# A first pair of feed-forward chunks by plain block products, with the input's sums made beside it

## The chip, the cores and the metric

One core of one Trainium2 chip runs the whole model. The metric is device time in microseconds (us); lower is better. All numbers are of the kernel before the change until the prediction ends.

## What is computed

The input x has 512 tokens of width 1024. It goes through two blocks of a first kind (feed-forward, attention mixture with pooling, feed-forward) and one block of a second kind (a mixing stage, then feed-forward). There are so five feed-forward layers, and each does this, with a width of 2816 between:

```python
def rmsnorm(x, g):
    xf = x.astype(jnp.float32)
    y = xf * lax.rsqrt(jnp.mean(xf * xf, axis=-1, keepdims=True) + NORM_EPS)
    return (y * g.astype(jnp.float32)).astype(x.dtype)

def swiglu(h, w_gate, w_up, w_down):
    return (jax.nn.silu(h @ w_gate) * (h @ w_up)) @ w_down
```

All data are float32, and the result is added to x (times 0.5 in the first four layers).

## The kernel before

x lies transposed in SBUF as eight tiles `x[0]` to `x[7]` of 128 channels by 512 tokens. TensorE multiplies in a 32-bit format that rounds, so every operand is split into a rounded high part and a low part (`wh`, `wl` for weights, `yh`, `yl` for the input), and one product is three matmuls: high by high, high by low, low by high. The high part is made on ScalarE (line 360 for weights), the low part on VectorE (line 368 for weights). The row factor of the norm is not put into the input: the sum of squares `ss` is made on the side (line 476, on POOL and VectorE), turned into a factor per token (`row_factor`: eight small matmuls `tst`, line 495, and eleven tiny VectorE steps, lines 484 to 497), spread over the partitions (`spread`: transposes `tbc`, line 506, and a copy into `rbc`, line 513), and multiplied into the gate and up results (line 575).

**A pair of chunks.** The width 2816 is 22 chunks of 128, taken in 11 pairs. For one pair, the weights (gate and up, two chunks) and the input (two halves of the 1024 channels, `x[0..3]` and `x[4..7]`, and two halves of the 512 tokens) form a 2 by 2 block product. It is done with seven half-size products, not eight, after Strassen and Winograd (`PRODUCTS`: W11, S1, S2, W12, S3, S4, W22). Each product is 24 matmuls of 256 columns (`product`, lines 628 to 630). For this the weights are summed on VectorE in `source` (lines 326, 330, 337, 341), and the input in `prep_a` (a difference of token halves for chunks 0 to 3, line 432) and `prep_b` (three sums `r` per chunk, lines 443 to 445, their high and low parts `rh`, `rl`, lines 447 and 450, and the split of chunks 4 to 7, lines 449 and 451). The seven results are put together by ScalarE snapshots (line 557), a ScalarE copy (line 595) and three VectorE adds (lines 606, 608, 610). Then `finish` scales a chunk by the row factor, applies SiLU, multiplies gate by up and splits the result into `ah`, `al`.

**The order.** `ffn_plan` lists the work: four phases of pairs, (0, 1), (2, 3, 4), (5, 6, 7), (8, 9, 10); the down-projections (`D`, eight per phase, line 600 adds them into x) of one phase are spread over the products of the next. The first phase so has two pairs with nothing beside them. The loop in `ffn` does one item after the other; after each it evacuates the item before and prepares weights two items ahead (`highs`, `lows`, `SPLIT = 2`). The row factor's statistics are issued after the third item, its spread after the fourth. A scheduler orders the instructions of each engine when the kernel is built, with the written order as priority; on the chip every engine then runs its queue in order.

**Where the input is prepared.** For the first layer `prep_a` and `prep_b` run ahead of everything. For layers behind a mixing stage, `prep_a` runs with the last output projection (`second`), and `prep_b` when the layer's pool opens (`layers`). The third layer follows a feed-forward layer directly: there both run as each x tile is finished (`next_ffn`).

**Buffers and queues.** Weights come by DMA on SyncE's queue into tiles `wr`, `wq`, `wd` (three buffers each); `wh` and `wl` have three buffers each, weight sums `wt` two, snapshots three. A feed-forward product writes one of PSUM's banks of tags x0, x1, x2, two buffers each.

Of the kernel before, what the change touches and what calls it, by code (L numbers as in the profile page):

```python
# [100 lines left out]
BLOCKS = {"W11": ((0, 0),), "S1": ((1, 0), (1, 1)), "W12": ((0, 1),)}  # L101

PHASES = ((0, 1), (2, 3, 4), (5, 6, 7), (8, 9, 10))
D_ORDER = (0, 4, 1, 5, 2, 6, 3, 7)


def ffn_plan():

    for ph, pairs in enumerate(PHASES):
        todo = [(ph, p, n) for p in pairs for n in PRODUCTS]  # L110
        ds = [(ph - 1, d) for d in D_ORDER] if ph else []
        for i, t in enumerate(todo):
# [107 lines left out]
def tile_blocks(tc, A, out):  # L220
# [3 lines left out]
    with (  # L224
# [46 lines left out]
        def home(m):  # L271

            j, _ = owner[m]
            name = PLAN[j][0]
            if name == "u":
                return "wr"
            if name in ("D", "W12"):
                return "wd"
            return "wq" if homes_of[j] % 2 else "wr"

        homes_of, n = {}, 0
        for j, (name, _) in enumerate(PLAN):
            if name == "u":
                n = 0
            elif name == "W11":
                n += 1
            homes_of[j] = n - 1
# [25 lines left out]
        def source(j):  # L313

            name, ws = PLAN[j]
            m = first_load[j]
            if name in ("u", "D"):
                return raws[m], ws[0], [m]
# [33 lines left out]
        def high(j):  # L352

            if PLAN[j][0] not in ("u", "W11") and state["ffn"] is None:
                return False
            if not loads(j):
                return False
            src, n, free = source(j)
            h = wspl.tile([P, 1024], F32R, name="wh", tag="wh")
            ACT.activation(h[:, :n], src[:, :n], AF.Copy)  # L360
            made[j] = src, n, free, h
            return True
# [64 lines left out]

        def prep_a(c, g):

            t = small.tile([P, S], F32, name="sq", tag="sq", bufs=2)  # L430
            ACT.activation(t, x[c], AF.Copy, scale=gain(g, c))
            V.tensor_sub(t[:, HALF:], t[:, :HALF], t[:, HALF:])
            h, l = new_pair(c)
            ACT.activation(h, t, AF.Copy)
            V.tensor_sub(l, t, h.bitcast(F32))  # L435

        def prep_b(c, g):

            b = state["ffn"].tile([P, 4, HALF], F32, name="b4", tag="cc", bufs=2)
            r = state["ffn"].tile([P, 4, HALF], F32, name="r3", tag="cc", bufs=2)[:, :3]  # L440
            ACT.activation(b[:, 0:2], x[c + 4], AF.Copy, scale=gain(g, c + 4))
            ACT.activation(b[:, 2:4], x[c], AF.Copy, scale=gain(g, c))
            V.tensor_sub(r[:, 1], b[:, 1], b[:, 3])
            V.scalar_tensor_tensor(r[:, 0], r[:, 1], -1.0, b[:, 2], op0=ALU.mult, op1=ALU.subtract)
            V.scalar_tensor_tensor(r[:, 2], r[:, 0], -1.0, b[:, 0], op0=ALU.mult, op1=ALU.subtract)
            h, l = rest[c] = [state["ffn"].tile([P, 3, HALF], F32R, name=f"r{e}{c}", tag=f"r{e}{c}", bufs=1) for e in "hl"]
            ACT.activation(h, r, AF.Copy)  # L447
            yh, yl = new_pair(c + 4)
            ACT.activation(yh, b[:, 0:2], AF.Copy)
            V.tensor_sub(l, r, h.bitcast(F32))  # L450
            V.tensor_sub(yl, b[:, 0:2], yh.bitcast(F32))

# [87 lines left out]
        def operand(name, c):  # L540

            if name in ("W11", "S1"):
                t, j = pair[c], name == "S1"
            elif name in ("W12", "S4"):
                t, j = pair[c + 4], name == "S4"
            else:
                t, j = [p.rearrange("p a b -> p (a b)") for p in rest[c]], ("S2", "S3", "W22").index(name)
            return cut(t, slice(None), slice(j * HALF, (j + 1) * HALF))

        def ffn(coef, nxt):  # L550
            pool = state["ffn"]
# [15 lines left out]

            def finish(f):

                t = cc.pop(f)  # L570
                g, u, hl = t[:, :, 0], t[:, :, 1], []
                rb = got["rb"].rearrange("p (a b) -> p a b", a=2)

                def one():
                    V.tensor_tensor(t, t, rb.unsqueeze(2).to_broadcast([P, 2, 2, HALF]), op=ALU.mult)
                    ACT.activation(g, g, AF.Silu)
# [20 lines left out]
            def evac(t, o):  # L597
# [11 lines left out]
                elif n == "S4":  # L609
                    V.tensor_add(flat(chunk(2 * p), 1), o[n], snap["S2"])  # L610
                    finish(2 * p)
                elif n == "W22":
                    finish(2 * p + 1)

            def rest_of():
# [5 lines left out]
            def product(o, w, n, start):  # L621
                for j in range(2):
                    for c in range(4):
# [6 lines left out]
                        PE.matmul(oo, wl, xh, start=False, stop=c == 3, skip_group_check=True)  # L630

            before = None
            highs(state["next"] + 3)
            lows(state["next"] + 3)
            o = {}
            for i, t in enumerate(ffn_plan()):
                w = take()
                if len(t) == 2:
# [4 lines left out]
                    for k, f in enumerate(ks):  # L643
                        mm3(od, cut(w, slice(None), slice(k * P, (k + 1) * P)), a[f], k == 0, k == len(ks) - 1)
                    now = t, od
                else:
                    n = t[2]
# [16 lines left out]
                before = now  # L664
                if i == 2:
                    r = row_factor(sums["s"], D, "rf")
                if i == 3:
                    got["rb"] = spread(r)
            evac(*before)


# [134 lines left out]
        def mix(l, nxt):  # L806
            with tc.tile_pool(name="mix", bufs=2) as pool:
# [153 lines left out]
                def second(d, o):  # L961
                    first(d, o)
                    square_x(d)
                    if d < 4:
                        prep_a(d, nxt)

# [85 lines left out]
        def mix2(nxt):  # L1052
            with tc.tile_pool(name="mix2", bufs=2) as pool:
# [166 lines left out]
                with tc.tile_pool(name="at", bufs=2) as at:  # L1220
# [273 lines left out]
                    def second(d, o):  # L1494
# [4 lines left out]
                        if d < 4:  # L1499
                            prep_a(d, nxt)  # L1500

# [15 lines left out]
        def layers(g=None):  # L1517
            with tc.tile_pool(name="ffn", bufs=2) as pool:
                state["ffn"] = pool
                if g is not None:  # L1520
                    for c in range(4):
                        prep_b(c, g)
                yield
                state["ffn"] = None

        def next_ffn(g):
            def f(d):
                if d < 4:
# [22 lines left out]
        with layers():  # L1551
            for c in range(4):
                prep_a(c, G_FFN1)
                if c == 0:
                    ahead(1)
            ahead(2)
            for c in range(4):
                prep_b(c, G_FFN1)
# [3 lines left out]
            ffn(0.5, next_mix(G_MIX))  # L1562
        mix(0, G_FFN2)
        with layers(G_FFN2):
            ffn(0.5, next_ffn(G_FFN1 + 1))
            ffn(0.5, next_mix(G_MIX + 1))
        mix(1, G_FFN2 + 1)
        with layers(G_FFN2 + 1):
            ffn(0.5, next_mix(G_PROD))
        mix2(G_FFN3)  # L1570
        with layers(G_FFN3):
            ffn(1.0, square_d)
        rb = spread_out(row_factor(sums["s"], D, "rf"))
# [22 lines left out]
```

## Time and profile before

| what | us |
|---|---|
| median of three runs (2571.61 to 2573.69) | 2573.45 |
| the profiled execution | 2572.86 |
| its span, first to last instruction | 2571.1 |
| TensorE (PE) busy | 2475.6 |
| VectorE (DVE) busy | 2003.3 |
| ScalarE (ACT) busy | 1345.3 |
| GpSimd (POOL) busy | 343.9 |

Busy time is the union of the times of an engine's instructions. Matmuls overlap in TensorE's pipeline, so one matmul's duration says less than the distance between two starts. The granted clock is given as a share of 2.4 GHz: 0.50 is 1.2 GHz. A VectorE instruction of 512 columns takes about 0.7 us in the trace and the next one starts about 0.6 us after it began. In the trace's names `x<-yh,wh` is a feed-forward product from a split input chunk, `x<-rh,wh` one from a sum of the input, `dn` a down-projection, `mm` a product of a mixing stage.

### The profile page before, as it was taken

The numbers are of one execution on the slowest core, as the hardware profiler recorded it, in microseconds if no ns is written. First come the engines' busy times: TensorE is split into PE (matmuls) and PEld (weight loads), VectorE is DVE, ScalarE is ACT, GpSimd is POOL, SyncE is SP. The second block draws the span as 40 slices with busy tenths as digits, with TensorE's granted clock in tenths as the row PEclk, the third lists the DMA queues.
The fourth block names the chain that finished last, engine by engine and source line by source line (L and its number), as shares of the span: only waits on it lengthen the run. The fifth ranks groups of instructions, "written<-read, shape, count | busy, mean of one in ns | idle before, by whom it ended". The sixth has DMA issues, their size and how long they took to land.

```text
span 2571.1 us, 40560 instructions
## 1 busy us (share of the span) xinstructions
PE 2475.6 (96%) x16074; PEld 2248.3 (87%) x16074; DVE 2003.3 (78%) x2935; ACT 1345.3 (52%) x2120; POOL 343.9 (13%) x498
## 2 busy tenths in 40 slices
PE   6999999998999999999999998999999999799997
PEld 5999988887999989999988887999987887799996
DVE  8887764788887779877756789887768888888775
ACT  5444443676544456444444776444455775554442
POOL 1000014431000000000023531000013553000001
PEclk9999999998999999999999998999999999799999
DMA  4333232212333332333232112333233211333322
GB/s 146 114 102 103 72 100 90 58 34 86 99 103 105 105 108 82 103 109 105 77 91 79 42 50 96 114 101 103 73 109 99 88 34 42 99 107 103 97 70 76
DMA packets 73342, 229.78 MB, mean 89 GB/s; under 512 B 9536, under 2 KB 9920, under 8 KB 73152
## 3 DMA queue, kind: packets, MB, share of 16 engines
q1 hardware_dynamic: 73152, 227.19, 29.1%
q8 instruction: 126, 2.06, 0.3%
q14 instruction: 64, 0.52, 0.1%
HBM read 225.06 MB, written 2.10 MB: 88 GB/s over the span
## 4 chain that ended last, share of the span: by engine, by line
PE 84%; DVE 10%; ACT 3%; issue 2%; POOL 1%; DMA 0%; DVEq 0%; SPq 0%; ACTq 0%; POOLq 0%
PE x L629 14%; PE x L630 14%; PE x L628 14%; PE dn L404 8%; PE dn L405 7%; PE dn L406 7%; PE mm L404 4%; PE mm L405 4%; PE mm L406 4%; DVE wl L368 2%; PE ov L1015 2%; PE tp L997 2%; PE mm L754 1%; PE mm L755 1%; PE ov L1292 1%
## 5 line engine op out<-in xcount | busy, mean ns | idle before, releaser
L628 PE MATMUL x<-yh,wh 128*128 128x256 f32 x1760 | 507.1, 288 | 20.2 <-ACT wh L360 14.1
L629 PE MATMUL x<-yl,wh 128*128 128x256 f32 x1760 | 506.8, 288 | 13.6 <-DVE yl L435 7.9
L630 PE MATMUL x<-yh,wl 128*128 128x256 f32 x1760 | 505.7, 287 | 3.7 <-DVE wl L368 3.7
L360 ACT ACTIVATE wh<-wd 128x768 fp32r<-128x768 f32 (+2 forms) x270 | 242.8, 899 | 358.2 <-PE x L629 178.7
L628 PE MATMUL x<-rh,wh 128*128 128x256 f32 x1320 | 377.2, 286 | 14.8 <-ACT rh L447 10.0
L629 PE MATMUL x<-rl,wh 128*128 128x256 f32 x1320 | 376.9, 286 | 4.0 <-DVE rl L450 4.0
L630 PE MATMUL x<-rh,wl 128*128 128x256 f32 x1320 | 376.0, 285 | 0.8 <-DVE wl L368 0.8
L628 PEld LDWEIGHTS x<-yh,wh 128*128 128x128 f32 x1760 | 344.2, 196 | 25.8 <-ACT wh L360 14.8
L629 PEld LDWEIGHTS x<-yl,wh 128*128 128x128 f32 x1760 | 344.3, 196 | 19.9 <-DVE yl L435 9.7
L630 PEld LDWEIGHTS x<-yh,wl 128*128 128x128 f32 x1760 | 344.7, 196 | 4.9 <-DVE wl L368 4.9
L404 PE MATMUL dn<-ah,wh 128*128 128x512 f32 x880 | 343.9, 391 | 0.0
L405 PE MATMUL dn<-al,wh 128*128 128x512 f32 x880 | 343.8, 391 | 0.0
L406 PE MATMUL dn<-ah,wl 128*128 128x512 f32 x880 | 342.3, 389 | 0.0
L360 ACT ACTIVATE wh<-wr 128x1024 fp32r<-128x1024 f32 (+1 forms) x178 | 187.7, 1055 | 244.1 <-PE x L629 89.9
L476 POOL TENSOR_TENSOR ss<-ss,sq 128x512 f32<-128x512 f32 x48 | 70.1, 1460 | 1807.6 <-ACT sq L475 1794.6
L368 DVE TENSOR_TENSOR wl<-wd,wh 128x768 fp32r<-128x768 f32 (+2 forms) x270 | 276.4, 1024 | 42.8 <-ACT wh L360 40.2
L628 PEld LDWEIGHTS x<-rh,wh 128*128 128x128 f32 x1320 | 255.4, 193 | 19.6 <-ACT rh L447 12.1
L368 DVE TENSOR_TENSOR wl<-wr,wh 128x1024 fp32r<-128x1024 f32 (+1 forms) x166 | 207.8, 1254 | 73.7 <-ACT wh L360 72.9
L629 PEld LDWEIGHTS x<-rl,wh 128*128 128x128 f32 x1320 | 255.4, 193 | 7.4 <-DVE rl L450 5.7
L630 PEld LDWEIGHTS x<-rh,wl 128*128 128x128 f32 x1320 | 255.5, 194 | 1.0 <-DVE wl L368 1.0
L600 DVE SCALAR_TENSOR_TENSOR x<-dn,x 128x512 f32<-128x512 f32 x160 | 110.0, 688 | 115.3 <-PE dn L406 115.3
L406 PEld LDWEIGHTS dn<-ah,wl 128*128 128x128 f32 x880 | 165.2, 188 | 35.3
(334 smaller groups left out, 5221.3 us busy)
## 6 DMA issues: line engine op xcount, KB each, us to landing
wr<-in_w SPq DMA_DIRECT2D x175, 512.0 KB, 3.6
wd<-in_w SPq DMA_DIRECT2D x120, 384.0 KB, 3.1
wq<-in_w SPq DMA_DIRECT2D x78, 512.0 KB, 3.6
wd<-in_w SPq DMA_DIRECT2D x55, 512.0 KB, 3.6
wd<-in_w SPq DMA_DIRECT2D x40, 256.0 KB, 2.9
x<-in_xT SPq DMA_DIRECT2D x8, 256.0 KB, 5.9
out<-x SPq DMA_DIRECT2D x8, 256.0 KB, 2.0
bias<-in_consts SPq DMA_DIRECT2D x2, 448.0 KB, 4.0
```

The lines of the kernel that those rows point to most:

```text
L360: ACT.activation(h[:, :n], src[:, :n], AF.Copy)
L368: state["low"] = eng.tensor_sub(l[:, :n], src[:, :n], h[:, :n].bitcast(F32)).ins
L404: PE.matmul(o, w[0], xx[0], start=start, stop=False)
L405: PE.matmul(o, w[0], xx[1], start=False, stop=False)
L406: PE.matmul(o, w[1], xx[0], start=False, stop=stop)
L476: eng.tensor_add(sums["s"], sums["s"], sq)
L600: V.scalar_tensor_tensor(x[d], o, coef, x[d], op0=ALU.mult, op1=ALU.add)
L628: PE.matmul(oo, wh, xh, start=start and j == 0 and c == 0, stop=False, skip_group_check=True)
L629: PE.matmul(oo, wh, xl, start=False, stop=False, skip_group_check=True)
L630: PE.matmul(oo, wl, xh, start=False, stop=c == 3, skip_group_check=True)
L997: PE.transpose(o[:, i * P : (i + 1) * P], prob[h * TC + i][0][:, j * P : (j + 1) * P], ident)
L1015: PE.matmul(o, w, part, start=(j == 0 and n == 0), stop=(j == TC - 1 and n == 1))
```

## The change

The first pair of every layer (pair 0) is done by four plain block products, T11, T12, T21, T22, in place of the seven. Each takes one weight block as loaded, with no sums, and a whole split half of the input: 24 matmuls of 512 columns into two banks (gate and up). T11 and T12 add into the same two banks, which give the first chunk; T21 and T22 give the second. `finish` scales straight out of these banks. The input is now split whole for all eight chunks (`split`), and `sums_of` makes four sums per chunk, with their high and low parts; it is called in `ffn` after each of the first four items, or, for the layer behind a feed-forward layer, in `next_ffn`. The weights of T11, T12 and T21 may be prepared before the layer's pool is open. The row factor's statistics are issued after the first item and the spread after the second.

```diff
+PLAIN = ("T11", "T12", "T21", "T22")
+BLOCKS.update({f"T{i + 1}{j + 1}": ((i, j),) for i in range(2) for j in range(2)})
...
-        todo = [(ph, p, n) for p in pairs for n in PRODUCTS]
+        todo = [(ph, p, n) for p in pairs for n in (PRODUCTS if p else PLAIN)]
...
-            if name in ("u", "D"):
+            if name in ("u", "D") or name in PLAIN:
                 return raws[m], ws[0], [m]
...
-            if PLAN[j][0] not in ("u", "W11") and state["ffn"] is None:
+            if PLAN[j][0] not in ("u", *PLAIN[:3]) and state["ffn"] is None:
                 return False
...
-        def prep_a(c, g):
...
-        def prep_b(c, g):
...
+        def sums_of(c, g):
+
+            b1, b2 = (state["ffn"].tile([P, 2, HALF], F32, name="b", tag="snap", bufs=3) for _ in range(2))
+            r = state["ffn"].tile([P, 4, HALF], F32, name="r", tag="wt", bufs=2)
+            ACT.activation(b1, x[c], AF.Copy, scale=gain(g, c))
+            ACT.activation(b2, x[c + 4], AF.Copy, scale=gain(g, c + 4))
+            V.tensor_sub(r[:, 0], b1[:, 0], b1[:, 1])
+            V.tensor_sub(r[:, 2], b2[:, 1], b1[:, 1])
+            V.scalar_tensor_tensor(r[:, 1], b2[:, 1], -1.0, r[:, 0], op0=ALU.mult, op1=ALU.subtract)
+            V.scalar_tensor_tensor(r[:, 3], r[:, 1], -1.0, b2[:, 0], op0=ALU.mult, op1=ALU.subtract)
+            h, l = rest[c] = [state["ffn"].tile([P, 4, HALF], F32R, name=f"r{e}{c}", tag=f"r{e}{c}", bufs=1) for e in "hl"]
             ACT.activation(h, r, AF.Copy)
...
             V.tensor_sub(l, r, h.bitcast(F32))
...
-            def finish(f):
+            def finish(f, banks=None):
...
                 def one():
+                    if banks:
+                        for w, b in zip((g, u), banks):
+                            V.tensor_tensor(w, b.rearrange("p (a b) -> p a b", a=2), rb, op=ALU.mult)
+                            if w is g:
+                                ACT.activation(g, g, AF.Silu)
+                        return
                     V.tensor_tensor(t, t, rb.unsqueeze(2).to_broadcast([P, 2, 2, HALF]), op=ALU.mult)
...
+                elif n in ("T12", "T22"):
+                    finish(n == "T22", o)
...
+            def plain(o, w, i, j):
+
+                for n in range(2):
+                    for c in range(4):
+                        m = 512 * n + c * P
+                        mm3(o[n], cut(w, slice(None), slice(m, m + P)), pair[4 * j + c], j == 0 and c == 0, j == 1 and c == 3)
...
+                elif t[2] in PLAIN:
+                    if i % 2 == 0:
+                        o = [xbank(j, "mm") for j in range(2)]
+                    plain(o, w, i // 2, i % 2)
+                    now = t, o
...
-                if i == 2:
+                if i == 0:
                     r = row_factor(sums["s"], D, "rf")
-                if i == 3:
+                if i == 1:
                     got["rb"] = spread(r)
+                if i < 4 and gain_of is not None:
+                    sums_of(i, gain_of)
...
                         if d < 4:
-                            prep_a(d, nxt)
+                            split(d, nxt)
...
                 if g is not None:
-                    for c in range(4):
-                        prep_b(c, g)
+                    for c in range(4, KC):
+                        split(c, g)
...
             def f(d):
-                if d < 4:
-                    prep_a(d, g)
-                else:
-                    prep_b(d - 4, g)
+                split(d, g)
+                if d >= 4:
+                    sums_of(d - 4, g)
                 square_d(d)
```

## Rows read from the trace of the kernel before

**Rows 1.** The page: busy us, share of the span, instructions.

```profile
PE 2475.6 (96%) x16074; PEld 2248.3 (87%) x16074; DVE 2003.3 (78%) x2935; ACT 1345.3 (52%) x2120; POOL 343.9 (13%) x498
```

**Rows 2.** Windows: stretch; length; PE, PEld, DVE, ACT, POOL busy (count); PEclk; DMA.

```profile
7.70:83.00 75.30, 60.56 (x411) 56.45 (x412) 72.57 (x122) 44.41 (x66) 8.21 (x5) 0.98 0.38 130
615.40:682.50 67.10, 57.75 (x414) 54.53 (x413) 61.13 (x83) 39.78 (x55) 2.81 (x2) 0.87 0.24 71
975.10:1029.30 54.20, 51.26 (x414) 50.29 (x413) 52.23 (x70) 33.46 (x46) 0.00 (x0) 1.00 0.26 79
1558.80:1625.40 66.60, 58.31 (x414) 55.08 (x413) 61.21 (x84) 39.85 (x55) 2.83 (x2) 0.87 0.24 72
2186.10:2262.60 76.50, 62.01 (x413) 58.62 (x412) 69.37 (x94) 45.41 (x64) 4.34 (x3) 0.82 0.31 100
626.40:643.40 17.00, 10.81 (x39) 8.83 (x39) 15.99 (x32) 7.72 (x11) 0.00 (x0) 0.50 0.18 60
```

**Rows 3.** Waits of PE, second and fifth window: us in total, times, longest.

```profile
PE x L628 <- ACT snap L557: 2.4, 1, 2.4
...
PE x L628 <- ACT rh L447: 4.8, 2, 3.5
```

**Rows 4.** Timeline of PE early in the first layer: start, duration, what.

```profile
17.15 0.41 PE L628 MATMUL x<-yh,wh 128*128 128x256 f32 x1
17.36 0.41 PE L629 MATMUL x<-yl,wh 128*128 128x256 f32 x1
```

**Rows 5.** Timeline of PE: first and last of two unbroken runs at full clock.

```profile
607.92 0.39 PE L404 MATMUL mm<-yh,wh 128*128 128x512 f32 x1
...
615.17 0.39 PE L406 MATMUL mm<-yh,wl 128*128 128x512 f32 x1
...
618.10 0.28 PE L630 MATMUL x<-yh,wl 128*128 128x256 f32 x1
...
621.70 0.28 PE L630 MATMUL x<-yh,wl 128*128 128x256 f32 x1
```

**Rows 6.** DVE by line, second window: busy, mean ns | idle before it.

```profile
L575 DVE TENSOR_TENSOR cc<-cc,rbc 128x1024 f32<-128x1024 f32 x4 | 4.9, 1220 | 0.0
L450 DVE TENSOR_TENSOR rl<-r,rh 128x768 fp32r<-128x768 f32 x4 | 3.8, 947 | 0.0
...
L368 DVE TENSOR_TENSOR wl<-wr,wh 128x1024 fp32r<-128x1024 f32 x3 | 3.6, 1217 | 1.5 <-ACT wh L360 1.5
...
L435 DVE TENSOR_TENSOR yl<-sq,yh 128x512 fp32r<-128x512 f32 x1 | 1.8, 1776 | 0.0
...
L959 DVE TENSOR_TENSOR x<-mm,x 128x512 f32<-128x512 f32 x2 | 1.4, 677 | 0.0
L443 DVE TENSOR_TENSOR r<-b 128x256 f32<-128x256 f32 x3 | 1.2, 410 | 0.0
```

**Rows 7.** Timeline: the factor's statistics, its copy in five layers, last adds of squares.

```profile
29.62 0.68 DVE L476 TENSOR_TENSOR ss<-ss,sq 128x512 f32<-128x512 f32 x1
...
55.40 0.59 ACT L513 COPY rbc<-tbc 128x512 f32<-128x512 f32 x1
...
622.43 0.68 DVE L476 TENSOR_TENSOR ss<-ss,sq 128x512 f32<-128x512 f32 x1
...
625.17 0.28 PE L495 MATMUL tst<-ones,ss 128*128 128x1 f32 x2
...
645.54 0.58 ACT L513 COPY rbc<-tbc 128x512 f32<-128x512 f32 x1
...
998.62 0.59 ACT L513 COPY rbc<-tbc 128x512 f32<-128x512 f32 x1 [0.76 <-PE tbc L506]
...
1588.38 0.58 ACT L513 COPY rbc<-tbc 128x512 f32<-128x512 f32 x1
...
2225.91 0.58 ACT L513 COPY rbc<-tbc 128x512 f32<-128x512 f32 x1
```

More of the change, by code (lines that the diff above doesn't have):

```diff
@@ L276, in home @@
                 return "wr"
-            if name in ("D", "W12"):
+            if name in ("D", "W12", "T22"):
                 return "wd"
@@ L284, in tile_blocks @@
                 n = 0
-            elif name == "W11":
+            elif name in ("W11", "T11"):
                 n += 1
@@ L426, in square_x @@
             square(x[c], c == 0, V if c >= KC - 2 else G)
-        def prep_a(c, g):
[L430 to L435, printed above, removed]
-        def prep_b(c, g):
[L439 to L446, printed above, removed]
+        def sums_of(c, g):
[8 more added lines that the diff above has]
+            h, l = rest[c] = [state["ffn"].tile([P, 4, HALF], F32R, name=f"r{e}{c}", tag=f"r{e}{c}", bufs=1) for e in "hl"]
             ACT.activation(h, r, AF.Copy)
-            yh, yl = new_pair(c + 4)
-            ACT.activation(yh, b[:, 0:2], AF.Copy)
             V.tensor_sub(l, r, h.bitcast(F32))
-            V.tensor_sub(yl, b[:, 0:2], yh.bitcast(F32))
         rest = {}
@@ L540, in operand, with ffn @@
         def operand(name, c):
[L542 to L545, printed above, removed]
+            if name in ("W11", "W12", "S4"):
+                t, j = pair[c if name == "W11" else c + 4], name == "S4"
             else:
-                t, j = [p.rearrange("p a b -> p (a b)") for p in rest[c]], ("S2", "S3", "W22").index(name)
+                t, j = [p.rearrange("p a b -> p (a b)") for p in rest[c]], ("S1", "S2", "S3", "W22").index(name)
             return cut(t, slice(None), slice(j * HALF, (j + 1) * HALF))
-        def ffn(coef, nxt):
+        def ffn(coef, nxt, gain_of=None):
             pool = state["ffn"]
@@ L566, in flat @@
                 return t[:, half].rearrange("p a b -> p (a b)")
-            def finish(f):
-                t = cc.pop(f)
+            def finish(f, banks=None):
+                t = chunk(f)
+                cc.pop(f)
                 g, u, hl = t[:, :, 0], t[:, :, 1], []
@@ L1499, in second @@
                         if d < 4:
-                            prep_a(d, nxt)
+                            split(d, nxt)
                     side, early, xn = beside(), {}, dict(pair)
@@ L1551, in tile_blocks @@
         with layers():
-            for c in range(4):
-                prep_a(c, G_FFN1)
+            for c in range(KC):
+                split(c, G_FFN1)
                 if c == 0:
@@ L1556, in tile_blocks @@
             ahead(2)
-            for c in range(4):
-                prep_b(c, G_FFN1)
             for c in range(KC):
@@ L1561, in tile_blocks @@
             rope_tables()
-            ffn(0.5, next_mix(G_MIX))
+            ffn(0.5, next_mix(G_MIX), G_FFN1)
         mix(0, G_FFN2)
         with layers(G_FFN2):
-            ffn(0.5, next_ffn(G_FFN1 + 1))
+            ffn(0.5, next_ffn(G_FFN1 + 1), G_FFN2)
             ffn(0.5, next_mix(G_MIX + 1))
@@ L1568, in tile_blocks @@
         with layers(G_FFN2 + 1):
-            ffn(0.5, next_mix(G_PROD))
+            ffn(0.5, next_mix(G_PROD), G_FFN2 + 1)
         mix2(G_FFN3)
         with layers(G_FFN3):
-            ffn(1.0, square_d)
+            ffn(1.0, square_d, G_FFN3)
         rb = spread_out(row_factor(sums["s"], D, "rf"))
```

## The prediction

> **What bounds the kernel now.** The page comes first: TensorE is busy 96% of the span, VectorE 78% [rows 1]. That average hides five short stretches, so the second view is the busy time by window, one window for the start of each feed-forward layer, from its first gate/up product to the first add of a down-projection result into x. Each window holds the same TensorE work: two pairs of chunks (14 products), two products of the third pair, one down-projection and the row statistics; its matmul counts are 411 to 414. Yet the lengths are 75.3, 67.1, 54.2, 66.6 and 76.5 us [rows 2]. In the third, the layer that follows another feed-forward layer, the clock is full and TensorE is busy 51.3 us. I take 51.3 as what the work itself costs. The excess is 24.0, 15.8, 2.9, 15.3 and 25.2 us, together 83.2 us. That is all the change can aim at.
>
> Who causes it? The waits of TensorE in these windows end, above all, on the rounded sums of the input and on a snapshot stuck behind such work on ScalarE [rows 3]. They are short, 2.4 and 3.5 us the longest of these, but inside the second window TensorE is granted 0.50, the 1.2 GHz level, for 17.0 us after such waits, and does only 39 matmuls there [rows 2]. In the same 17.0 us VectorE is busy 15.99. So VectorE sets the pace: it must make sums of the input, sums of the weights and low parts of both before TensorE can run on. In the first window the matmuls stand 0.21 us apart, against 0.12 at full clock [rows 4, 5].
>
> **The change, part by part.** *TensorE.* Thirty 256-column matmuls take 3.60 us (618.10 to 621.70), 0.120 us each; thirty-two of 512 columns take 7.25 us (607.92 to 615.17), 0.227 each [rows 5]. A pair by seven products is 168 x 0.120 = 20.2 us; by four plain ones it is 96 x 0.227 = 21.8. The change adds 1.6 us per layer, 8.2 in all; nothing hides it where TensorE does not wait. The Trainium skill, "TensorE: Matmul & The Clock Gate", Back-to-back issue gap, gives a full-clock gap of N/2.4 + 2.5 ns. By it, as an estimate, the pairs would cost 18.4 and 20.7 us, 2.4 more per layer, and the sum below would end 4 us later. The spacing in rows decides.
>
> *VectorE, removed per layer.* Three low parts of weights (1.22 each), four weight sums (same shape, 1.22), three evacuation adds (0.68, as the add that takes another bank into x), four 256-wide subtractions in the first halves' preparation (0.41, priced like the same shape of the sums): 3.7 + 4.9 + 2.0 + 1.6 = 12.2 us [rows 6]. *Added:* a fourth sum per input chunk, 4 x 0.41 = 1.6; the low part of the sums grows from 768 to 1024 columns, 0.95 to 1.22, 4 x 0.27 = 1.1; scaling straight out of four half-chunk banks, which I price like the evacuation adds that also read a bank, 4 x 0.68 against 2 x 1.22: 0.3. Net 9.2 us less. The input's split for all eight chunks stays (one operation with the gain in place of a subtraction, same width).
>
> *ScalarE* drops three weight roundings and four snapshots or copies, and gains a little in the sums; it has 27 us free in the second window [rows 2], so I cost it at nothing. If that cover were gone, three roundings of about 1 us come back. *Queues:* the load order and the number of loads stay; weights of plain products are released sooner, so SyncE issues no later. POOL's squares are unmoved.
>
> *Moved:* the sums of the four input chunk pairs (some 2.9 us of VectorE each: 4 x 0.41 + 1.22) now run beside the plain products, and all four stand ahead of the next pair's second product. After the first product TensorE's in-order queue gets the statistics products, after the second the transposes that spread the row factor; before, they stood behind the third and fourth of seven shorter products.
>
> **The sum.** TensorE's floor per window becomes 51.3 + 1.6 = 52.9. VectorE's load decides whether that is reached.
> - Second window: VectorE is busy 61.1 now [rows 2]. Inside it I take off three low parts 3.7, two weight sums 2.4 (the other two ran before it), evacuations 2.0, put on 3.0, and let 2.4 us move ahead of it (a split of 1.8 and one add of 0.7 that VectorE was late with [rows 6]): 53.6. VectorE idles 2.0 us even in the third window, so I add 1.8: 55.4, a gain of 11.7. The fourth likewise: 11.2.
> - Fifth: 69.4 - 4.9 (four low parts) - 4.9 - 2.0 - 0.8 + 3.0 = 59.8, with waits 61: gain 15.5.
> - First: 72.6 - 3.7 - 4.9 - 2.0 - 1.2 + 3.0 = 63.8, with waits 66: gain 9.3. TensorE alone would need 52.9 plus the first 24 matmuls at the low clock, where 256 columns take 0.21 and 512 so 0.43, 24 x 0.20 = 4.8: 57.7, less.
> - Third: its sums are made beside the down-projection before it, as now; TensorE's floor 52.9 and 0.6 of wait give 53.5, a gain of 0.7.
>
> Together 48.4 us. The profiled execution took 2572.9 us (span 2571.1 and 1.8 around it), 0.6 below the median of the runs; 2572.9 - 48.4 = 2524.5. My own range for this case is 2508 to 2542: 3 us either way in each of the five windows, rounded up. From no change one can tell about 0.2%, 5 us.
>
> **The unknown wait.** No row shows how fast the row factor gets through once its statistics stand earlier. In the second window the statistics products start at 625.17, the copy of the spread factor at 645.54 [rows 7], 20 us later: the factor's eleven tiny VectorE steps queue between large ones. Now the plain products hold two banks until that factor is there, and the next pair's first product needs one of them back. After the copy come 0.6 for itself, 1.4 for two scalings, then seven products, two more and the down-projection (20.2 + 5.8 + 2.7) and 0.3: about 31 us to the window's end. Lower bound: the copy is early by the 4 us by which the statistics move up (a first plain product takes 5.4 us from 615.4), so 641 + 31 = 672, a window of 57, 1.6 over my 55.4. Upper bound: it lands where it lands now. I take the first end, since less work now stands between the tiny steps; the other is a rival. A second wait is possible ahead of it: the statistics need the last add of squares, which ended at 623.1 in the second window [rows 7], and the first plain product ends at 620.9. TensorE's queue would stand, with the second plain product behind it, 2 us there and in the fourth and fifth. In the first window that add ended at 30.3, and a first product at the low clock, 24 x 0.43 from 7.8, ends near 18: up to 12 us. The ends are nothing and 18 us in all. I take nothing, since the weight sums and the input's sums that were queued ahead of those adds are gone or behind them; the other end, 2543, is in the range.
>
> **Rivals.**
> - *TensorE alone binds.* VectorE keeps up everywhere. For it: the third window comes near it with VectorE busy 52.2 of 54.2 us [rows 2]. Windows of 57.7 and four of 52.9: a gain of 339.7 - 269.3 = 70, 2502.5. Against: VectorE was the pace. Chance 0.11.
> - *The sums come too late.* The next pair's second product needs the low parts of all four sums. From 615.4 VectorE has 21.8 + 2.9 = 24.7 us for 4 x 2.9 of sums, four low parts and one weight sum (5 x 1.22), four adds and splits of 0.68 and a chunk's finish of four such: 23.1, without the factor's steps. If two sums are left at that point, four layers lose 5.8 us each: 2548. Chance 0.09.
> - *The row factor holds the banks: the slower side.* If the copy lands where it lands now (55.40, 645.54, 998.62, 1588.38, 2225.91 [rows 7]) each window ends 31 us behind it: 3.4 later, 6.0 earlier, 0.3 later, 6.0 and 5.7 earlier, 14 us of gain, 2559. For every us that it lands later still, five are lost: it turns at 2.8 us, and at 5 us late the time is 2584. For it: sums of the input now compete with the tiny steps. Against: seven large VectorE operations of the old first pair are gone. Chance 0.03 for 2559, 0.04 for 2584.
> - *The busiest engine gets more work.* The idle time only moves behind the first pair, where VectorE would be as late as now, and the extra matmuls come on top: 2572.9 + 8.2 = 2581. Against it stands the 9.2 us that leave VectorE. The Trainium skill, "Perfetto Trace Analysis", Identifying Performance Opportunities, looks for gains in the most-contended engine's own work; by occupancy that is TensorE, and the change lengthens it. Chance 0.02.
> - *The change does nothing*: the order of instructions is chosen when the kernel is built, and it may still put the sums ahead of the plain products; then early waits stay and the 9.2 us of VectorE just pay for the matmuls, 2573. Chance 0.01.
>
> **How the numbers follow.** Forecast 0.70. Faster: 0.70 + 0.11 + 0.09 + 0.03 = 0.93; I keep 0.01 of it back for an order I cannot see: 0.92. Same 0.02, slower 0.06. The range 2506 to 2550 takes in the forecast's own range and the late sums, and leaves out most of the first rival, the bank case and the slower side.
>
> **What the changed profile would show.** Right: windows from the first plain product to the first down-projection add near 66, 55, 53.5, 55 and 61 us; no stretch at 0.50 in the second and fourth; VectorE some 9 us per layer less; 512-column matmuls 0.227 apart. Wrong: a TensorE wait on the spread factor or on a bank ahead of the second pair (the banks' rival), a wait on the low parts of the sums at its second product (the late sums), or windows near 53 (TensorE alone).

## The result, and the profile after

The changed kernel takes 2528.82 us (median of 4 runs, 2527.74 to 2532.32) against 2572.83 us for the kernel before (4 runs, 2571.61 to 2573.69). The ratio is 0.9832 with a 95% interval of 0.9815 to 0.9849: 44 us faster. The forecast was 2524.5 in 2506 to 2550. The profiled execution of the kernel after took 2529.62 us, with a span of 2527.8.

First the page's busy line of the kernel after, the answer to [rows 1].

```profile
PE 2462.2 (97%) x15714; PEld 2217.4 (88%) x15714; DVE 1964.1 (78%) x2895; ACT 1315.2 (52%) x2065; POOL 343.9 (14%) x498
```

VectorE lost 39.2 us of work, TensorE 13.4 us of busy time, although it got longer products: its busy time counts matmuls at the low clock at their longer duration, and there are fewer of these now. Next the windows of the kernel after, cut in the same way as [rows 2] (from the first product of a layer to its first down-projection add); the last two lines are the parts of the first layer's window with a granted clock of 0.50, the 1.2 GHz level.

```profile
7.60:77.71 70.11, 62.85 (x343) 53.88 (x344) 64.59 (x115) 38.96 (x55) 9.19 (x5) 0.90 0.40 140
608.70:663.80 55.10, 52.91 (x342) 47.88 (x342) 53.05 (x79) 34.23 (x45) 0.33 (x1) 1.00 0.26 77
956.70:1012.40 55.70, 53.46 (x342) 47.76 (x342) 48.01 (x66) 29.27 (x39) 0.00 (x0) 1.00 0.24 76
1541.80:1596.90 55.10, 52.94 (x342) 47.91 (x342) 53.06 (x79) 34.26 (x45) 0.32 (x1) 1.00 0.25 77
2158.30:2219.70 61.40, 55.33 (x342) 49.27 (x342) 59.69 (x88) 38.11 (x51) 4.97 (x3) 0.97 0.34 116
25.50:32.30 6.80, 6.80 (x19) 5.54 (x20) 5.80 (x21) 4.34 (x6) 0.00 (x0) 0.50 0.57 187
49.40:56.20 6.80, 6.37 (x27) 5.48 (x26) 6.80 (x7) 3.61 (x5) 0.00 (x0) 0.50 0.26 78
```

In the first window the clock figures of both kernels leave out a slow start, which the rows count as full clock (1.00 for 7.6 to 14.0 us of the kernel after); the durations of single matmuls show it. The first line is of the kernel before and the second of the kernel after; at full clock these two sizes take 0.28 and 0.39 us.

```profile
28.53 0.41 PE L630 MATMUL x<-yh,wl 128*128 128x256 f32 x1
...
11.22 0.63 PE L409 MATMUL mm<-yh,wl 128*128 128x512 f32 x1
```

Matmuls take that long until 28.9 us in the kernel before and until 11.8 us in the kernel after. So the first window begins with 21 us at the low clock before the change and with 4 after it; the pace of 0.21 us that the prediction put to VectorE's work there [rows 4] is this clock's.

The windows were 75.3, 67.1, 54.2, 66.6 and 76.5 [rows 2]; they are 70.0, 55.0, 55.6, 55.0 and 61.3 (the rows' edges lie up to 0.1 outside). Together 339.7 became 297.0, a gain of 42.7 of the span's 43.3. So the whole gain is at the starts, as forecast. In the second and fourth window the clock is full, where [rows 2] had 17.0 us at 0.50, and TensorE is busy 52.9 of 55.1.

What TensorE still waits for, by window: first, second, third and fifth, in this order (the fourth is as the second; engine, tile and line, what released it; us in total, times, longest). They answer to [rows 3].

```profile
PE tst L487 <- DVE pf L710: 2.7, 1, 2.7
PE x L627 <- ACT rh L442: 1.8, 1, 1.8
...
PE x L628 <- DVE rl L443: 0.9, 1, 0.9
...
PE tst L487 <- DVE ss L468: 1.3, 1, 1.3
PE tbc L498 <- DVE rf L481: 0.9, 1, 0.9
...
PE tst L487 <- DVE ss L468: 1.1, 1, 1.1
PE mm L408 <- DVE yl L456: 1.0, 1, 1.0
...
PE mm L408 <- DVE yl L456: 2.5, 1, 2.5
PE x L627 <- ACT rh L442: 2.0, 1, 2.0
PE x L628 <- DVE rl L443: 1.4, 1, 1.4
```

Three kinds are seen. `tst` and `tbc` are the row factor's statistics and its spread: TensorE's queue stands there until the last add of squares, or the factor, is done. (In the first line the releaser named, `pf`, is a tiny instruction right behind the last add of squares.) `rh` and `rl` are the input's sums, late at the second product of the next pair; this is only in the first and fifth window. `yl` is the low part of a split input chunk, which the plain products themselves need: 1.0 us in the third window, 2.5 in the fifth, and 1.4 in the first, in three waits not shown.

The timeline of the kernel after shows the plain products' pace and the factor's way (start, duration, what; the answers to [rows 4, 5, 7]).

```profile
29.03 0.63 PE L407 MATMUL mm<-yh,wh 128*128 128x512 f32 x1
29.45 0.63 PE L408 MATMUL mm<-yl,wh 128*128 128x512 f32 x1
...
615.68 1.05 PE L487 MATMUL tst<-ones,ss 128*128 128x1 f32 x8 [1.32 <-DVE ss L468]
...
617.14 0.40 PE L409 MATMUL mm<-yh,wl 128*128 128x512 f32 x1
...
625.34 0.39 PE L409 MATMUL mm<-yh,wl 128*128 128x512 f32 x1
...
628.19 0.58 ACT L505 COPY rbc<-tbc 128x512 f32<-128x512 f32 x1 [3.35 <-PE tbc L498]
```

From 617.14 to 625.34 are 36 matmuls of 512 columns, 0.228 us each, as taken from [rows 5]; at the low clock they stand 0.42 apart. The statistics start 7.0 us into the second window (615.68 - 608.70) and the spread factor is copied 19.5 us into it. Before, it was 9.8 and 30.1 us [rows 2, 7]. The way from the one to the other, with its tiny VectorE steps (twelve in the trace), takes 12.5 us, where it took 20.4.

### The profile page after: what moved, and what is told of

Its sections match the earlier page's. It is cut to its first block, busy times and chain, and to the rows that moved or that the text cites. A ratio compares the mean times of both kernels' runs of the same rounds, so it can differ in the third digit from the quotient of the medians.

```text
span 2527.8 us, 39773 instructions
## 1 busy us (share of the span) xinstructions
PE 2462.2 (97%) x15714; PEld 2217.4 (88%) x15714; DVE 1964.1 (78%) x2895; ACT 1315.2 (52%) x2065; POOL 343.9 (14%) x498
## 4 chain that ended last, share of the span: by engine, by line
PE 84%; DVE 10%; ACT 3%; issue 2%; POOL 1%; DMA 1%; SPq 0%; DVEq 0%; ACTq 0%; POOLq 0%
PE x L629 13%; PE x L628 13%; PE x L627 13%; PE dn L407 8%; PE dn L408 8%; PE dn L409 8%; PE mm L407 5%; PE mm L408 5%; PE mm L409 4%; DVE wl L371 2%; PE ov L1028 2%; PE tp L1010 1%; PE mm L767 1%; PE mm L768 1%; DVE yl L456 1%
## 5 line engine op out<-in xcount | busy, mean ns | idle before, releaser
L627 PE MATMUL x<-rh,wh 128*128 128x256 f32 x1600 | 454.6, 284 | 4.0 <-ACT rh L442 3.8
L628 PE MATMUL x<-rl,wh 128*128 128x256 f32 x1600 | 454.6, 284 | 2.3 <-DVE rl L443 2.3
L629 PE MATMUL x<-rh,wl 128*128 128x256 f32 x1600 | 454.6, 284 | 0.0
L627 PE MATMUL x<-yh,wh 128*128 128x256 f32 x1200 | 339.7, 283 | 0.3 <-ACT wh L363 0.3
L628 PE MATMUL x<-yl,wh 128*128 128x256 f32 x1200 | 339.7, 283 | 0.0
L629 PE MATMUL x<-yh,wl 128*128 128x256 f32 x1200 | 339.6, 283 | 0.0
L628 PEld LDWEIGHTS x<-rl,wh 128*128 128x128 f32 x1600 | 308.7, 193 | 5.0 <-DVE rl L443 2.7
L627 PEld LDWEIGHTS x<-yh,wh 128*128 128x128 f32 x1200 | 230.2, 192 | 3.2 <-ACT wh L363 0.9
L628 PEld LDWEIGHTS x<-yl,wh 128*128 128x128 f32 x1200 | 230.3, 192 | 2.3
L629 PEld LDWEIGHTS x<-yh,wl 128*128 128x128 f32 x1200 | 230.1, 192 | 0.0
```

The lines of the kernel that those rows point to most:

```text
L627: PE.matmul(oo, wh, xh, start=start and j == 0 and c == 0, stop=False, skip_group_check=True)
L628: PE.matmul(oo, wh, xl, start=False, stop=False, skip_group_check=True)
```

## The experiments

Each was timed beside the kernel before, in one of four groups, whose medians of the kernel before were 2573.41, 2572.90, 2572.97 and 2572.39 us. "Window" is always as above.

**The place of the sums.** All sums of the input run ahead of the plain products.

```diff
-                if i < 4 and gain_of is not None:
-                    sums_of(i, gain_of)
...
                     for c in range(4, KC):
                         split(c, g)
+                    for c in range(4):
+                        sums_of(c, g)
...
```

> The changed kernel (2528.8 us), but the sums of the input are written ahead of the plain products again (after the splits, when the layer's pool opens); everything else stays. If it is the order of VectorE's work that gave the time (the splits and low parts that the plain products need come ahead of 11.4 us of sums), four layers lose 6 to 11 us each: 2553 to 2572. If it is VectorE's total alone, 9.2 us less per layer wherever the sums stand, each layer loses at most 3: 2529 to 2541.

Measured: 2549.88 us (2548.64 to 2552.02), ratio 0.991 [0.9896, 0.9923]; 21 us of the 44 are lost. The work is the same. Windows of this kernel, and its waits over the whole span:

```profile
7.50:82.80 75.30, 63.06 (x341) 55.00 (x342) 66.13 (x114) 39.12 (x55) 12.29 (x5) 0.89 0.37 130
613.70:673.60 59.90, 55.63 (x343) 50.40 (x342) 53.52 (x79) 34.38 (x45) 0.34 (x1) 0.94 0.23 71
...
1552.80:1610.10 57.30, 53.03 (x342) 47.84 (x341) 53.34 (x79) 34.31 (x45) 0.25 (x1) 1.00 0.24 74
2171.00:2240.90 69.90, 58.82 (x342) 52.76 (x342) 60.39 (x88) 38.42 (x51) 4.97 (x3) 0.88 0.30 102
```

```profile
PE tbc L498 <- DVE rf L481: 18.5, 5, 7.2
PE tst L487 <- DVE ss L468: 8.8, 5, 3.0
...
PE x L627 <- DVE cc L568: 5.8, 4, 1.6
```

In the second window VectorE is busy 53.5 us, as in the kernel after (53.05), and yet the window is 4.8 us longer. Of these, 2.1 are waits: TensorE idles 4.3 us and not 2.2. The rest is its low clock (0.94), which the fourth window does not show: there the same waits at full clock make 2.3 us. So in these two the load of VectorE is not what sets the length; the place of the work is. With the sums queued first, the factor's tiny steps come late: TensorE waits at `tbc`, and after that the next pair's first product waits for a scaling to give a bank back (`cc`, in four of the five layers). Most of the loss is in the first and fifth window, 5.1 and 8.4 us, where the waits at `tbc` are 5.5 and 7.2; the third loses nothing. (The five `tbc` waits in the fence are four of these windows and one of 2.4 us at the norm behind the last layer, which the kernel after has too.)

**The statistics one product later.** Issued after the second plain product, not the first, with the spread right behind.

```diff
-                if i == 0:
+                if i == 1:
                     r = row_factor(sums["s"], D, "rf")
```

> The changed kernel, with the row factor's statistics written after the second plain product instead of the first. If the waits of TensorE on the last add of squares ahead of the statistics (2.9, 1.5, 1.3 and 1.5 us in four layers of the changed kernel's trace) are real losses, they are now covered by 5.4 us of product: 4 to 7 us faster, 2522 to 2525. If the factor then holds the two banks that the next pair needs, up to 3 us per layer are lost in their place: 2529 to 2544.

Measured: 2529.57 us (2529.07 to 2530.59), 0.9831 [0.9817, 0.9844], no difference. In the second window the 1.3 us at `tst` went and the 0.9 at `tbc` became 2.0. The second fence is the first window:

```profile
PE tbc L498 <- DVE rf L481: 2.0, 1, 2.0
```

```profile
7.50:73.50 66.00, 58.13 (x344) 49.74 (x345) 64.47 (x115) 38.81 (x54) 9.20 (x5) 1.00 0.41 149
```

The first and third window became 4.1 and 0.7 us shorter, the second, fourth and fifth 1.9, 0.3 and 0.8 longer. TensorE's idle time changed by at most 0.7 us in any of them; in the first it even grew, from 7.2 to 7.9 us. What made that window shorter is the clock: no stretch at 0.50 behind the slow start, where the kernel after has 13.6 us. The second is longer by its clock too (0.97).

**The statistics where they were in the list.** After the third plain product, and the spread after the fourth; `finish` then reads the factor later.

```diff
...
-                if i == 0:
+                if i == 2:
                     r = row_factor(sums["s"], D, "rf")
-                if i == 1:
+                if i == 3:
                     got["rb"] = spread(r)
...
```

> The changed kernel, but with the row factor's statistics after the third plain product and its spread after the fourth, where the kernel before had them in its list of items (third and fourth). If the earlier place is part of what was gained (the plain products' banks wait for the factor, the bank rival): TensorE waits for a scaling or a bank ahead of the second pair's first products in most layers, 3 to 6 us in each, 2540 to 2560. If the statistics' place is worth nothing, since the tst waits of 1.3 to 2.9 us go and pay for the later factor: 2524 to 2533.

Measured: 2546.64 us (2544.88 to 2553.02), 0.9906 [0.9889, 0.9922]: 17.8 us lost. Windows, waits of the span, and the timeline of the second window:

```profile
607.40:670.40 63.00, 56.17 (x342) 50.49 (x342) 54.15 (x79) 34.39 (x45) 0.34 (x1) 0.92 0.22 68
...
1549.40:1612.40 63.00, 56.20 (x342) 50.59 (x342) 54.12 (x79) 34.40 (x45) 0.31 (x1) 0.92 0.22 67
```

```profile
PE tbc L498 <- DVE rf L481: 21.6, 5, 5.9
PE x L626 <- DVE cc L567: 8.7, 5, 2.2
```

```profile
636.10 1.12 PE L498 MATMUL tbc<-consts,rf 128*128 128x128 f32 x4 [5.04 <-DVE rf L481]
...
637.26 0.59 ACT L505 COPY rbc<-tbc 128x512 f32<-128x512 f32 x1 [4.43 <-PE tbc L498]
...
638.62 0.58 PE L626 MATMUL x<-yh,wh 128*128 128x256 f32 x1 [1.40 <-DVE cc L567]
```

This is the rival of the held banks, in the open: the factor is copied 29.9 us into the window, as in the kernel before (30.1); TensorE stands 5.0 us for it and 1.4 more for a scaling. The window ends 33 us behind the copy (31 were forecast). By time the statistics are later than they were before, since a plain product is longer: they start 17.1 us into this window, against 9.8. The second and fourth window pay 7.9 us each, 4.6 of it in idle time and the rest at the low clock (0.92). The other three pay 1.3 in sum, and not because the factor is in time there: the wait for a scaling (`cc`) comes once in each of the five layers. In the first and fifth it stands in place of the late sums.

**The early statistics alone**, in the kernel before.

```diff
-                if i == 2:
+                if i == 0:
                     r = row_factor(sums["s"], D, "rf")
-                if i == 3:
+                if i == 1:
                     got["rb"] = spread(r)
```

> The kernel before, with the statistics after the first product and the spread after the second, as the change has them, and nothing else changed. If the early statistics alone gave part of the gain: 2550 to 2566. If they give nothing without the plain pair, because there the first scaling is not due before the first pair's last products: 2570 to 2578; slower than that if TensorE's queue now stands at the statistics while the last adds of squares are still behind the sums, with 3 to 8 us in each of layers 1, 2, 4 and 5: 2580 to 2600.

Measured: 2574.84 us (2572.09 to 2578.91, 10 runs), 1.0009 [1.0, 1.0019]. They give nothing by themselves: the old first pair does not need the factor before its last products. In the second window the copy lands 27.4 us in, 2.7 earlier than before, and the window is still 1.7 us longer. The wait at the statistics is new there:

```profile
PE tst L495 <- DVE ss L476: 2.8, 1, 2.8
```

**The plain pair alone:** the sums first and the statistics late, both edits in one.

> The plain first pair alone: all four sums ahead of the plain products as in the run with the sums first, and statistics and spread after the third and fourth product as in the run with late statistics. If the plain pair is worth its time only by the places that it leaves free for the other work (sums 21.1 us, statistics 17.8 us, each measured alone), and these add: 2528.8 + 38.9 = 2567.7, in 2562 to 2573. If the 9.2 us of VectorE that each layer loses are worth much by themselves (two layers' 11 us and two more of 9 to 15): 2530 to 2545. If the two places hide one another (the late factor hides late sums' wait): 2548 to 2558.

Measured: 2559.14 us (2557.83 to 2560.54), 0.9948 [0.9932, 0.9965], a gain of 13.3. So the two places are worth 30.3 of the 44 us (2559.14 - 2528.82). One by one they measured 21.1 and 17.8; they overlap, since both show as the same wait, 18.5 and 21.6 us alone and 23.9 together, where the kernel after has 4.2:

```profile
PE tbc L498 <- DVE rf L481: 23.9, 5, 7.1
PE x L626 <- DVE cc L567: 8.0, 5, 2.2
```

Both places act through one chain, the row factor's: each of the five layers waits for a scaling, and each window ends 32 to 33.4 us behind the factor's copy. In the kernel after that distance is 35.6 to 40.1 us.

**Less VectorE work: one sum for four.** This kernel leaves out the sums of three of the four chunk pairs.

```diff
         def sums_of(c, g):
+            if c:
+                rest[c] = rest[0]
+                return
```

> The changed kernel with the sums of the first input chunk alone, used in place of those of the other three: three quarters of the sums' work are left out, 8.6 us of VectorE per layer. If the sums still lie on the path in the first and fifth layer only, the time falls by 9 to 14 us, 2515 to 2520, and the second to fourth layer's windows stay within 1.5 us of 55. If VectorE's load binds in every layer, each falls by 2 to 8: 2500 to 2512. If the sums are wholly hidden: 2526 to 2529.

Measured: 2520.43 us (2517.53 to 2524.93), 0.9796 [0.9783, 0.9809]. Its second and fourth window, and what TensorE waits for in each of the two:

```profile
603.60:659.80 56.20, 54.38 (x344) 49.19 (x343) 46.38 (x63) 28.06 (x37) 0.52 (x1) 0.97 0.24 76
...
1537.20:1594.80 57.60, 55.82 (x342) 50.40 (x341) 46.15 (x62) 27.83 (x37) 0.40 (x1) 0.94 0.23 74
```

```profile
PE tst L490 <- DVE ss L471: 1.8, 1, 1.8
```

VectorE has 6.7 us less to do in the second window and the window is 1.1 us longer; the fourth is 2.5 longer. TensorE idles 1.8 us in both, where it was 2.2; what makes them longer is its low clock behind that wait (0.97 and 0.94). So 7 us less of VectorE take 0.4 us of waits away in these two. The profiled execution is the slowest of the four (2524.93). The gain is in the first, third and fifth (4.6, 3.3, 2.6): where sums were late, or, in the third, made beside the work ahead.

**Less VectorE work in the kernel before.** This one leaves out the weight sums of the first pair: its products take loaded blocks as they are.

```diff
...
-                V.tensor_add(t, t, raws[g["11"]])
+                if lead(j) not in FIRST:
+                    V.tensor_add(t, t, raws[g["11"]])
...
-                V.tensor_add(t, t, g["s2"])
+                if lead(j) not in FIRST:
+                    V.tensor_add(t, t, g["s2"])
...
```

> The kernel before, with the first pair's four weight sums left out in every layer (the four products that need a sum use one weight block as loaded). TensorE and ScalarE do the same work, the input's sums stay ahead of the products; VectorE has 4.9 us less per layer. If VectorE's load sets the pace of these starts, four layers gain 4 to 5 us and the third 1 to 2: 2551 to 2557. If the place of the input's sums alone sets it, little comes back, under 6 us in all: 2567 to 2573.

Measured: 2564.33 us (2563.47 to 2566.91), 0.9968 [0.9956, 0.998], between the two theories. VectorE is 1.8 to 4.1 us less busy in each window; the second and fourth follow (67.1 to 64.2, 66.6 to 64.0), the fifth by less than half (76.6 to 74.9, for 4.0 us of work), the first not at all (76.3). TensorE's idle time fell in all five, by 2.7, 2.9, 1.0, 2.0 and 0.3 us; in the first and third window more time at the low clock took that back:

```profile
7.50:83.90 76.40, 64.30 (x413) 60.02 (x414) 70.73 (x119) 44.73 (x66) 8.25 (x5) 0.89 0.39 130
613.30:677.60 64.30, 57.86 (x415) 54.52 (x414) 58.02 (x81) 39.60 (x55) 2.89 (x2) 0.89 0.26 74
```

**The price of a plain pair**, by a second one in mid-layer (pair 6), where nothing waits.

```diff
-        todo = [(ph, p, n) for p in pairs for n in (PRODUCTS if p else PLAIN)]
+        todo = [(ph, p, n) for p in pairs for n in (PLAIN if p in (0, 6) else PRODUCTS)]
...
```

> The changed kernel, with the seventh pair of every layer plain too. It lies in the middle of the layer, where TensorE does not wait, so it measures TensorE's price of a plain pair by itself. By the spacing of matmuls in the trace, 0.227 and 0.120 us, it is 1.6 us per layer: 2529 + 8 = 2537. By a gap of N/2.4 + 2.5 ns (Trainium skill, TensorE: Matmul & The Clock Gate) it would be 2.4: 2541. If VectorE's relief counts there as well, under 2533.

Measured: 2540.44 us (2535.47 to 2542.16), 0.9871 [0.9857, 0.9884]. The rest of the third layer (first to last down-projection add), in the kernel after and in this one:

```profile
1012.30:1305.20 292.90, 292.90 (x1979) 272.22 (x1979) 222.56 (x245) 134.61 (x177) 7.48 (x6) 1.00 0.32 96
```

```profile
1011.80:1306.30 294.50, 294.50 (x1908) 270.11 (x1908) 213.26 (x237) 129.88 (x170) 7.49 (x6) 1.00 0.32 95
```

TensorE is busy throughout at full clock in both, and the difference is 1.6 us, as it is in the other layers. By five layers that is 8 us; the runs are 11.6 slower in the median, the profiled one 5.9, and the rest is not settled.

**A second plain pair at the start** (pairs 0 and 1 of every layer).

```diff
-        todo = [(ph, p, n) for p in pairs for n in (PRODUCTS if p else PLAIN)]
+        todo = [(ph, p, n) for p in pairs for n in (PLAIN if p in (0, 1) else PRODUCTS)]
...
```

> The changed kernel, with the second pair of every layer plain too, so that the sums have 44 us of products to hide behind. TensorE pays another 1.6 us per layer, 8.2 in all. If the waits ahead of the second pair's second product in the first and fifth layer (3.8 and 3.7 us, and the low clock after them, some 5 more) are the sums coming too late, they go, and the sum is 2524 to 2532. If they have another cause, TensorE's 8 us are added: 2535 to 2538.

Measured: 2529.27 us (2526.93 to 2530.38), 0.9828 [0.9814, 0.9841]. The windows are 65.1, 57.5, 57.5, 57.0 and 60.3: 5.0 and 1.1 shorter in the first and fifth, where the sums get more time, and 1.9 to 2.5 longer in the others, for 1.6 us of TensorE and no sums that were late.

**By layer.** So the second plain pair goes to the first and fifth layer alone, and the statistics stand after the second product in the third.

```diff
+PLAINS = (2, 1, 1, 1, 2)
+MID = (2,)
...
-                if i == 0:
+                if i == (layer in MID):
...
```

> The changed kernel, with two plain pairs in the first and fifth layer, where the sums came late, one in the others, and the row factor's statistics after the second product in the third layer. From the ends of the five starts in the traces of the kernels that had each part: 5.3 us less in the first, 0.7 in the third, 1.0 in the fifth: 2522, within 2519 to 2526. If those differences came from where the low clock happened to fall in single runs: 2527 to 2531.

Measured: 2520.10 us (2517.43 to 2523.31), 0.9796 [0.9782, 0.9809]. A second form has the later statistics in the first layer too (`MID = (0, 2)`).

> As the one with two plain pairs in the first and fifth layer, but the statistics come after the second product in the first layer too. There TensorE waited 2.8 us for the statistics behind the first product. If that wait goes without another in its place: 1 to 3 us less than the other, about 2520. If the order only moves it: the same within 1 us.

Measured: 2519.39 us (2517.07 to 2520.62), 0.9791 [0.9778, 0.9804]. The two can't be told apart; both are some 9 us faster than the kernel after. The second form's windows:

```profile
7.50:71.00 63.50, 60.52 (x272) 49.15 (x273) 57.84 (x108) 34.12 (x48) 8.82 (x5) 0.97 0.44 155
599.90:655.00 55.10, 52.95 (x342) 47.90 (x342) 53.05 (x79) 34.27 (x45) 0.30 (x1) 1.00 0.25 77
...
2150.30:2209.00 58.70, 56.26 (x273) 47.44 (x273) 51.66 (x81) 33.60 (x44) 4.95 (x3) 0.97 0.36 121
```

## Why the prediction was right, and where not

**Size and sign: right.** 2524.5 was forecast and 2528.82 came; the gain is at the five starts and nowhere else.

**TensorE's price: right.** The plain pair costs 1.6 us per layer, in the trace's spacing (0.228 against 0.120) and in the mid-layer run. The Trainium skill, "TensorE: Matmul & The Clock Gate", Back-to-back issue gap, gives the formula N/2.4 + 2.5 ns for a single isolated matmul, and the estimate from it was 2.4 per layer; the run does not agree with that, and the measurement decides.

**VectorE's work: right.** Busy 64.6, 53.05 and 59.7 us in the first, second and fifth window, forecast 63.8, 53.6 and 59.8. Over the span it lost 39.2 us where five times 9.2 is 46; of the second window's VectorE lines, the answer to [rows 6], two prices held (1.22 for a low part of the sums, 0.68 for a scaling out of a bank), and one of the four additions per input chunk took 0.69, not 0.41:

```profile
L443 DVE TENSOR_TENSOR rl<-r,rh 128x1024 fp32r<-128x1024 f32 x4 | 4.9, 1220 | 0.0
...
L439 DVE SCALAR_TENSOR_TENSOR r<-b,r 128x256 f32<-128x256 f32 x4 | 2.8, 690 | 0.0
...
L568 DVE TENSOR_TENSOR cc<-mm,rbc 128x512 f32<-128x512 f32 x4 | 2.6, 684 | 0.0
```

**The windows: three hit, two mis-sized.** The second, fourth and fifth came at 55.0, 55.0 and 61.3 (55.4, 55.4, 61). The first is 70.0, not 66, and the third 55.6, not 53.5; these two are some 6 us, and the profiled execution missed the forecast by 5.1 us. The step that failed there is "I take nothing" for the second wait, TensorE's queue at the statistics. It measured 2.7, 1.3, 1.1 and 1.3 us in the first four windows. In the third, 1.1 of it and 1.0 for a late low part (`yl`) make most of the difference. In the first, the late sums (1.8 and 0.9) and the input's low parts (1.4) come on top, and the low clock: TensorE is busy 62.9 us there, 10 more than the 52.9 that full clock would need, over the slow start and the 13.6 us around these waits. The term "with waits 66" holds nothing for that clock. In the run with the statistics one product later, without those 13.6 us, the same window took 66.0 us with no less idle time, so what such waits cost by the clock differs between the two, and no run here shows why.

**The step that was wrong, though its number held: "VectorE's load decides whether that is reached."** In the kernel after it does not, in the second and fourth window. These are TensorE's 52.9 us and two waits, 1.3 at `tst` and 0.9 at `tbc`: 55.1. That VectorE is busy 53.05 of them is not the cause: with 46.4 the window still had 1.8 us of waits, and with 53.5 in another order it had 4.3 (56.2 and 59.9 us long, both with some low clock). So it is in part luck that a forecast of 55.4, built on VectorE's 53.6, came to 55.0. What decides is when two chains are done: from the last add of squares through the factor to the scaling that frees a bank, and from the input to the low parts of its sums. In the kernel before the load did count in these two windows, nearly one for one (3.2 us less work and 2.9 us less time in the second, 3.3 and 2.5 in the fourth), in the fifth by less than half, and in the first in TensorE's waits alone.

So the gain splits otherwise than I wrote it. I gave it to 9.2 us of VectorE per layer. Shown by the runs: 13.3 us come with the plain pair itself, 8 us of extra matmuls already paid, and 30.3 with the two places which it leaves open, for the sums beside the plain products and for the statistics at the front. Both places bring the row factor forward. The second place is worth nothing without the plain pair (1.0009).

**The rivals.** *The row factor holds the banks* is a true mechanism, and this change comes out of it by its early statistics and by the place of the sums: in the run that puts the statistics back, the copy lands where it landed before in the second and fourth window, as that rival had it (29.9 and 29.8 us into them, against 30.1 and 29.6). It was priced at 2559 and measures 2546.6: TensorE waits for a scaling in all five layers, but in the first and fifth the copy lands 35.7 and 29.8 us into the window, where it was 47.6 and 39.8. I had the copy early by 4 us at best; it is early by 10.6 (30.1 to 19.5), of which 2.8 is the earlier start and the rest the shorter queue between the tiny steps. *The sums come too late* is true in part, in the first and fifth layer; two plain pairs there bring most of the 9 us of the runs by layer. *TensorE alone binds*: not reached here; in the run with one sum only the third window came there (52.3 us), the second and fourth still wait at the statistics, although VectorE has 9 us and more to spare. *The busiest engine gets more work*: false here. The Trainium skill, "Perfetto Trace Analysis", Identifying Performance Opportunities, says that improving a kernel generally means improving the performance of the most-contended engine, and has the reader find the gaps on that engine. The trace agrees as to the gaps and not as to the engine's own work: TensorE's work grew by 8 us, its idle time fell in all five windows (from 9.4 to 2.2 us in the second), and the time fell by 44.

**Open:** how the 13.3 us of the plain pair alone divide between fewer operations on VectorE, its later need of the sums and the relief of ScalarE is not shown. ScalarE was costed at nothing, but it is busy 34.2 us in the second window and not 39.8, and the 2.4 us for which TensorE stood there for a snapshot [rows 3] are gone. The excess of the mid-layer run is open as well.

## What to carry to other kernels

When a stage starts with a chain of preparation, ask first what the first consumer needs, and give it work that needs none of the chain, even at the price of more work on the busiest engine; then move the chain beside that work. Look then for the next chain that ends in a shared buffer (here the row factor, which frees PSUM banks): it must move up too, or it takes back part of the gain (17.8 of 44 us here). Compare two orders of the same work before you conclude from an engine's busy share that its load is the limit.

## What was not expected of the hardware

Short waits of TensorE cost more than their own length in some cases and not in others. In the kernel after, the second and fourth window have waits of 1.3 and 0.9 us and keep a granted clock of 1.00. In the run with one sum, the fourth has a single wait of 1.8 us and then this stretch:

```profile
1544.90:1551.70 6.80, 6.80 (x20) 5.64 (x20) 5.77 (x17) 2.00 (x2) 0.00 (x0) 0.50 0.48 144
```

These are 13 matmuls of 512 columns and seven of the statistics' small ones. TensorE is busy 55.8 us in this window and 52.9 in the kernel after, for the same products: the clock adds some 3 us to a wait of 1.8. No run here isolates what decides between the two.
